# Mamba-2 SSD blocks: decay differences and order mask by TensorE into PSUM, dt on x, eight heads per vector operation

## The chip, the cores and the metric

The program runs on one core of one Trainium2 chip. The metric is the device time of an execution in microseconds. The kernel before took 2283.06 us, the median of three runs (2283.03 to 2285.35).

The core's engines are named as in the profile: PE (TensorE, matrix products; PEld is its loading of weights), DVE (VectorE, element by element), ACT (ScalarE, functions such as exp, and copies), POOL (GpSimd, element by element) and SP (SyncE, which issues the DMAs here). Each works through its own instructions in a fixed order. SBUF is the memory that all of them read; PE writes into PSUM, in banks of 512 fp32 columns.

## What is computed

A backbone of two layers over 512 latent tokens with a prefix of 256 context tokens, `D_MODEL` 1024. The first layer has latent attention and RWKV heads, the second Mamba-2 SSD heads beside windowed attention; each has a ConvFFN after it. The change concerns the SSD scan of the second layer: 16 heads of width 64, in two groups of 8 that share B and C (128 states), both directions in time, chunks of 128 tokens (2 of context, 4 of latents).

```python
a_cum = jnp.cumsum(dtc * a, axis=2)
tri = jnp.tril(jnp.ones((SSD_CHUNK, SSD_CHUNK), bool))
seg = a_cum[:, :, :, None] - a_cum[:, :, None, :]
decay_qk = jnp.exp(jnp.where(tri[:, :, None, None], seg, -jnp.inf))
cb = jnp.einsum('bcqgn,bckgn->bcqkg', cc, bc)
y_diag = jnp.einsum('bcqkgh,bckghp->bcqghp', cb[..., None] * decay_qk * dtc[:, :, None], xc)
decay_end = jnp.exp(a_cum[:, :, -1:] - a_cum)
chunk_states = jnp.einsum('bcqgn,bcqgh,bcqghp->bcghpn', bc, decay_end * dtc, xc)
...
y_off = jnp.einsum('bcqgn,bcghpn,bcqgh->bcqghp', cc, h_in, jnp.exp(a_cum))
y = (y_diag + y_off).reshape(b, l, SSM_HEADS, SSM_P)
```

`y_diag` is the part within a chunk: per head a 128x128 matrix of C·B, times the decay from token k to token q where k is not after q, times `dt` of k. `y_off` is the part from earlier chunks: the state `h_in` at the start of the chunk, read by C and scaled by the decay since then. The direction backwards in time does the same on reversed tokens.

## The kernel before

Activations lie with features on partitions and tokens along the rows. A dense product of the second layer's input projection (`dense`, whose matmuls have line 267, in the helper `mm`) takes a weight tile split into a high and a low part in fp32r (`whi`, `wlo`) and the activations split likewise (`hh`, `hl`), and makes three products per 128 rows of the contraction. The weight tiles are loaded ahead by `load_w` (DMA L322, `whi` on ACT L325, `wlo` on POOL or DVE L326).

PSUM has eight banks in this layer: the pool `acc` with two slots of 1024 columns (two banks each), `sd` with three banks and `b` with one. The dense products of the projections take an `acc` slot; `conv5` (ACT L1225, DVE L1229, SiLU on ACT L1232) drains it, and `token_major` (PE L1238, ACT L1239) transposes the result into `xtm`, x with tokens on partitions.

`decays()` (L1241 to L1279) projects dt for all 32 head-directions onto 48 partitions, makes `ac`, the cumulative decay exponents by two scans (L1257, L1258), and stores them in DRAM as `acd` (L1260). It also makes `dtm` and `acm`, dt and the exponents with tokens on partitions, and `wgt` and `dec` for the states between chunks.

Then, for each group g of 8 heads: four projections of x (`j`); the chain of states over chunks in both directions (`xw` on POOL L1320, a product on PE, `hn` on DVE L1328 and L1330); `cb`, the products of B and C, copied out of PSUM once per direction and multiplied by the mask `le` or `ge` (DVE L1341); and then, for each of the 4 latent chunks c, this (abridged, with the line numbers of the profile):

```
1348  dma(e, acd[c, h0:h0 + 8] broadcast to 128 partitions)
1351  act(gc, e, AF.Exp)
1352  ptt(out=gc, in0=gc, in1=cf[g][:, ls] for 8 heads, op=ALU.mult)
1354  for h in range(8): ts(out=e[:, h], in0=e[:, h], scalar1=acm[...], op0=subtract, op1=min 0)
1356  act(e, e, AF.Exp)
1359  for h in range(8): stt(out=e[:, h], in0=e[:, h], scalar=dtm[...], in1=cb, mult, mult)
```

once for each direction d. A tile of `E` is 128 tokens k by 8 heads by 128 tokens q; a tile of `G` is C with the decay since the chunk's start on it, for 8 heads. Per head, PE then adds four products into one bank of `sd`: for each direction `hn` with `G` (the part from earlier chunks) and `xtm` with `E` (the part within the chunk), each with an output of 64 partitions, the even heads on the lower half and the odd ones on the upper. DVE adds the bank into the output `ym` (L1371). `E` has four buffers, `G` four.

After both groups come the keys, values and queries of the windowed attention (rotary shuffles by DMA, POOL L1383, DVE L1384, L1385, L1390), the gate z (ACT L1548, DVE L1550), and the windowed attention itself.

The order of the instructions on each engine isn't the order of the source. A planner that knows a cost for every instruction sorts them when the program is built: what can start early by its estimate goes early, within the buffers that each tag has. So exponentials of `E` stand on ACT before the projections of x, dense products stand on PE between the SSD products, and the queries' projections and part of the gate's lie among the SSD blocks of group 1. Once built, the order on each engine is fixed; an instruction that isn't ready holds back all that stand behind it.

Of the kernel before, what the change touches and what calls it, by code (L numbers as in the profile page):

```python
# [10 lines left out]
F32 = mybir.dt.float32  # L11
# [6 lines left out]
P = 128  # L18
# [110 lines left out]
def layout(inp):  # L129
# [74 lines left out]
    a["scan2"] = cs["scan2"]  # L204
    a["const1"] = np.concatenate([cs["le"], cs["ge"]], 1)
# [5 lines left out]
def hybrid_kernel(ctx: ExitStack, tc: tile.TileContext, a, out):  # L211
# [1029 lines left out]
    def decays():  # L1241
# [18 lines left out]
        dma(acd.rearrange("c h t -> h c t"), ac[H48].rearrange("p (c t) -> p c t", t=P))  # L1260
        aed = tc.dram_tile([6, 48], F32, name="sp_ae")
# [17 lines left out]
        return acm, wgt, dec, dtm, acd  # L1279

    if DTJ < 0:
        acm, wgt, dec, dtm, acd = decays()
# [20 lines left out]
    seq = ([0, 1, 2, 3, 4, 5], [1, 0, 5, 4, 3, 2])  # L1303
    for g in range(2):
        for j in range(4 * g, 4 * g + 4):
            if j == DTJ:
                acm, wgt, dec, dtm, acd = decays()
# [7 lines left out]
        for d in range(2):  # L1315
            hprev = None
            hs = slice(32 * d + 8 * g, 32 * d + 8 * g + 8)
            for i, c in enumerate(seq[d][:-1]):
                xw = T("sw", [P, 512], "xw", 2)
# [18 lines left out]
        for c in range(2, 6):  # L1338
            for d in range(2):
                cbs[c, d] = T("sw", [P, P], "cb", 8)  # L1340
                tt(out=cbs[c, d], in0=b[:, (c - 2) * P:(c - 1) * P], in1=ge if d else le, op=ALU.mult)  # L1341
        for c in range(2, 6):
            ls = slice((c - 2) * P, (c - 1) * P)
            E, G = [], []
            for d in range(2):
                h0 = 32 * d + 8 * g
                e = T("sw", [P, 8, P], "E", 4)
                dma(e.rearrange("p h t -> p (h t)"),
                    acd[c, h0:h0 + 8].rearrange("h t -> (h t)").unsqueeze(0).partition_broadcast(P))
                gc = T("sw", [P, 8, P], "G", 4)  # L1350
                act(gc, e, AF.Exp)  # L1351
                ptt(out=gc, in0=gc, in1=cf[g][:, ls].unsqueeze(1).to_broadcast([P, 8, P]), op=ALU.mult)
                for h in range(8):
                    ts(out=e[:, h], in0=e[:, h], scalar1=acm[:, c, h0 + h:h0 + h + 1], scalar2=0.0, op0=ALU.subtract,  # L1354
                       op1=ALU.min)
                act(e, e, AF.Exp)
                cb = cbs[c, d]
                for h in range(8):
                    stt(out=e[:, h], in0=e[:, h], scalar=dtm[:, c, h0 + h:h0 + h + 1], in1=cb, op0=ALU.mult,
                        op1=ALU.mult)  # L1360
                E.append(e)
                G.append(gc)
# [263 lines left out]
```

## Time and profile before

| what | value |
|---|---|
| median of three runs | 2283.06 us |
| the profiled execution | 2277.27 us |
| its span, first to last instruction | 2275.6 us |
| mean granted clock of PE | 0.955 |
| PE busy | 2103.0 us |
| DVE busy | 1348.8 us |
| ACT busy | 927.6 us |
| POOL busy | 497.1 us |
| `E` subtractions on DVE (L1354) | 128, 61.1 us |
| `G` products on POOL (L1352) | 16, 39.9 us |
| `E` products on DVE (L1359) | 128, 35.0 us |
| loads of `E` on SP (L1348) | 16 of 512 KB, median 6.6 us to landing |

All times in views of the trace are counted from the start of the span of one profiled execution. A group of instructions is given as line, engine, operation, tiles (written, then read), count, then busy time, the mean of one in ns, and the engine's idle time just before them with what ended it. In a view of stretches each row has a start and an end, its length, the busy time of each engine with the number of instructions, the granted clock of PE (1.00 is full speed) and what the DMA did. An fp32 matmul stands in the trace as two records, an fp32r one as one. In the span the decay blocks of group 0 lie from about 1531 to 1604 us, those of group 1 from about 1643 to 1704 us.

### The profile page before, as it was taken

To read this page: it belongs to the slowest core of one execution; us is meant where nothing else is said; L and a number is where in the kernel's file an instruction comes from. 1 tells how busy PE (TensorE), PEld (TensorE's weight loads), DVE (VectorE), ACT (ScalarE), POOL (GpSimd) and SP (SyncE) were. 2 spreads that over 40 slices of the span, in tenths; PEclk is the share of its full clock that TensorE was granted. 3 is DMA by queue.
4 is the path that set the end of the run, shared out by engine and by line. 5 is a ranking of instruction groups with operands and counts; after the bars stand their busy time and mean duration, and the time that the engine had idled before them with its cause. 6 is when DMAs were issued, how large, how long until landed. Compare 5 with 4: busy or idle time off the path is not lost.

```text
span 2275.6 us, 33862 instructions
## 1 busy us (share of the span) xinstructions
PE 2103.0 (92%) x13558; PEld 1654.7 (73%) x13558; DVE 1348.8 (59%) x2081; ACT 927.6 (41%) x1434; POOL 497.1 (22%) x484
## 2 busy tenths in 40 slices
PE   5988899798899999999999998898888999999997
PEld 3666668686555778888888886786565667888886
DVE  5466865666677556445354454678975556554555
ACT  4345663532245244223132335544344345332434
POOL 0027586621133010000000004342641230000000
PEclk9899899699999999999999999999888999999999
DMA  8477677659861432221211223313426032223231
GB/s 307 110 196 200 176 207 200 208 161 313 256 225 42 148 133 71 61 66 56 74 53 59 75 60 112 97 48 116 132 66 170 31 105 84 93 94 101 84 116 61
DMA packets 181069, 282.58 MB, mean 124 GB/s; under 512 B 63328, under 2 KB 118656, under 8 KB 177840
## 3 DMA queue, kind: packets, MB, share of 16 engines
q1 hardware_dynamic: 180912, 280.42, 40.7%
q8 instruction: 107, 1.75, 0.3%
q14 instruction: 50, 0.41, 0.1%
HBM read 225.43 MB, written 47.33 MB: 120 GB/s over the span
## 4 chain that ended last, share of the span: by engine, by line
PE 64%; DVE 6%; DMA 4%; ACT 4%; issue 2%; SPq 0%; DVEq 0%; POOL 0%; ACTq 0%; POOLq 0%
PE acc L267 49%; PE sd L267 3%; PE wo L267 2%; PE b L267 2%; PE ab L267 2%; PE o L267 2%; DVE E L1354 1%; DMA u<-sp_v 1%; DMA E<-sp_ac 1%; PE ax L267 1%; ACT L416 0%; DMA f<-sp_q 0%; DMA wraw<-w_out 0%; PE mb L267 0%; PE ad L267 0%
## 5 line engine op out<-in xcount | busy, mean ns | idle before, releaser
L267 PE MATMUL acc<-s,whi 128*128 128x512 f32 (+1 forms) x3104 | 762.3, 356 | 2.4 <-ACT s L463 2.4
L267 PEld LDWEIGHTS acc<-s,whi 128*128 128x128 f32 x3104 | 545.1, 188 | 94.3 <-ACT s L463 6.1
L267 PE MATMUL acc<-s,wlo 128*128 128x512 f32 (+1 forms) x1552 | 460.6, 357 | 0.0
L267 PE MATMUL acc<-h,whi 128*128 128x256 f32 (+2 forms) x1248 | 321.6, 371 | 15.4 <-ACT p L635 4.9
L325 ACT CAST whi<-wraw 128x1024 fp32r<-128x1024 f32 (+5 forms) x228 | 210.2, 923 | 284.3 <-PE acc L267 203.9
L267 PEld LDWEIGHTS acc<-s,wlo 128*128 128x128 f32 x1552 | 290.5, 188 | 46.7 <-DVE wlo L326 0.7
L267 PEld LDWEIGHTS acc<-h,whi 128*128 128x128 f32 (+1 forms) x1248 | 223.0, 196 | 67.9 <-issue 15.6
L326 DVE TENSOR_TENSOR wlo<-wraw,whi 128x1024 fp32r<-128x1024 f32 (+5 forms) x205 | 219.2, 1072 | 40.0 <-ACT whi L325 39.4
L381 DVE SCALAR_TENSOR_TENSOR s<-acc,pv,s 128x511 f32<-128x511 f32 (+1 forms) x132 | 87.0, 659 | 245.3 <-ACT s L380 244.4
L380 ACT ACTIVATE s<-acc,pv 128x512 f32<-128x512 f32 (+1 forms) x132 | 93.5, 708 | 231.8 <-PE acc L267 220.5
L484 DVE SCALAR_TENSOR_TENSOR x<-acc,mods,x 128x512 f32<-128x512 f32 (+1 forms) x136 | 79.4, 621 | 176.5 <-PE acc L267 176.4
L267 PE MATMUL acc<-h,wlo 128*128 128x256 f32 (+2 forms) x624 | 179.8, 362 | 0.0
L434 POOL TENSOR_TENSOR f<-f,f 128x768 f32<-128x768 f32 (+1 forms) x24 | 31.3, 1305 | 629.9 <-ACT f L429 622.4
L267 PEld LDWEIGHTS acc<-h,wlo 128*128 128x128 f32 (+1 forms) x624 | 120.3, 196 | 21.7 <-issue 5.2
L383 DVE SCALAR_TENSOR_TENSOR s<-acc,pv,s 128x511 f32<-128x511 f32 (+1 forms) x132 | 87.2, 660 | 4.3
L1173 POOL TENSOR_TENSOR s<-w,s 128x256 f32<-128x256 f32 x6 | 5.0, 857 | 382.4 <-ACT s L416 382.4
L387 ACT CAST s<-s 128x768 fp32r<-128x768 f32 (+1 forms) x44 | 32.0, 727 | 109.4 <-DVE s L1146 109.4
L744 POOL TENSOR_TENSOR w<-I 128x30 f32<-128x30 f32 (+14 forms) x120 | 69.8, 582 | 30.7 <-PE iv L267 12.9
L326 POOL TENSOR_TENSOR wlo<-wraw,whi 128x1024 fp32r<-128x1024 f32 x23 | 62.8, 2734 | 58.5 <-ACT whi L325 55.0
L746 POOL TENSOR_TENSOR I<-I,w 128x30 f32<-128x30 f32 (+14 forms) x120 | 71.9, 599 | 9.1
L1354 DVE TENSOR_SCALAR E<-E,acm 128x128 f32<-128x128 f32 x128 | 61.1, 546 | 16.9 <-ACT G L1351 16.9
L719 DVE TENSOR_TENSOR W<-gk,con 64x512 f32<-64x512 f32 x48 | 32.8, 683 | 55.9 <-ACT PB L718 55.5
(389 smaller groups left out, 3375.0 us busy)
## 6 DMA issues: line engine op xcount, KB each, us to landing
aw<-ada SPq DMA_DIRECT2D x96, 512.0 KB, 6.1
wraw<-up SPq DMA_DIRECT2D x88, 512.0 KB, 3.5
rec<-sp_rec SPq DMA_DIRECT2D x24, 1024.0 KB, 11.4
wraw<-w_in SPq DMA_DIRECT2D x47, 512.0 KB, 3.8
wraw<-down SPq DMA_DIRECT2D x40, 384.0 KB, 3.1
sp_rec<-tg SPq DMA_DIRECT2D x24, 384.0 KB, 3.4
E<-sp_ac SPq DMA_DIRECT2D x16, 512.0 KB, 6.6
x<-xT SPq DMA_DIRECT2D x16, 384.0 KB, 6.0
```

The lines of the kernel that those rows point to most:

```text
L267: ins = nc.tensor.matmul(o, lhsT=lhsT, rhs=rhs, start=start, stop=stop, skip_group_check=shared)
L325: nc.scalar.copy(hi[:, :kt], raw[:, :kt])
L326: (eng or tt)(out=lo[:, :kt], in0=raw[:, :kt], in1=hi[:, :kt].bitcast(F32), op=ALU.subtract)
L380: act(o[rows, t0:t0 + n], ps[rows, po:po + n], AF.Identity, scale=w1, bias=b)
L381: stt(out=o[rows, t0 + 1:t0 + n], in0=ps[rows, po:po + n - 1], scalar=w0, in1=o[rows, t0 + 1:t0 + n], op0=ALU.mult, op1=ALU.add)
L383: stt(out=o[rows, t0:t0 + n - 1], in0=ps[rows, po + 1:po + n], scalar=w2, in1=o[rows, t0:t0 + n - 1], op0=ALU.mult, op1=ALU.add)
L387: nc.scalar.copy(hi, src)
L484: stt(out=x[:, t0:t0 + n], in0=ps[:, po:po + n], scalar=mods[:, c6 * 8 + m, c:c + 1], in1=x[:, t0:t0 + n], op0=ALU.mult, op1=ALU.add)
L719: tt(out=w[hk], in0=b[hk].rearrange("p c (a t) -> p c a t", a=2), in1=mk[hk].rearrange("p (a t) -> p a t", a=2).unsqueeze(1).to_broadcast( ...
L744: eng.tensor_tensor(out=tmp, in0=I[:, m + 1:, m:m + 1].to_broadcast([P, n, m]), in1=I[:, m:m + 1, :m].to_broadcast([P, n, m]), op=ALU.mult)
L746: eng.tensor_tensor(out=I[:, m + 1:, :m], in0=I[:, m + 1:, :m], in1=tmp, op=ALU.add)
L1354: ts(out=e[:, h], in0=e[:, h], scalar1=acm[:, c, h0 + h:h0 + h + 1], scalar2=0.0, op0=ALU.subtract, op1=ALU.min)
```

## The change

- **Decay differences by PE.** `lk[d]` holds 18 rows: the exponents of the 8 heads over the latent tokens, as a high and a low part in fp32r (16 rows, loaded once per group), and two rows of ones. `rq[d]` holds 18 rows by 8 heads by 128 tokens: -1 where a row belongs to the head (a constant, `sel`), and in the last two rows the exponents of the chunk, high and low part, loaded for each chunk and direction. Their product is the difference of the exponents for 8 heads, made in two halves of 512 columns in an `acc` slot.
- **Order mask by PE.** A second product into the same columns, of the identity with `drop[d]`, adds -1e30 where k is after q (before q in the other direction). The exponential is read by ACT straight from PSUM, over 1024 columns. `cb` is copied once per chunk, without a mask.
- **dt on x.** POOL makes `xd`, x times dt, for each chunk and direction; the 8 products by dt on `E` become one of `E` with `cb` over 1024 columns on DVE.
- **Decay of the part from earlier chunks on its products.** `hn` is multiplied with C once for two heads (four products of 128 columns into a bank `z` of `sd`); DVE multiplies the bank by the decays `eg`, which are loaded as a broadcast over 64 partitions for the even and the odd heads and put through an exponential of 512 columns on ACT. The two directions are added on DVE and added into `ym`. `G` is gone.
- **Buffers.** `E` has three, `eg` two, `rq` and `lk` one for each direction, `xw` three, shared by the chain of states and `xd`; `cb` four.
- **In `decays()`** the exponents are split into two fp32r parts and stored in DRAM (`parts`).

```diff
@@ decays() @@
         dma(acd.rearrange("c h t -> h c t"), ac[H48].rearrange("p (c t) -> p c t", t=P))
+        parts = tc.dram_tile([2, 48, NTOK], F32, name="sp_acp")
+        phi, plo = F(F32R), F(F32R)
+        nc.scalar.copy(phi[H48], ac[H48])
+        tt(out=plo[H48], in0=ac[H48], in1=phi[H48].bitcast(F32), op=ALU.subtract)
+        for x, t in enumerate((phi, plo)):
+            dma(parts[x], t[H48].bitcast(F32))
...
@@ before the loop over groups @@
+    idr = T("sw", [P, P], "idr", 1, F32R)
+    nc.scalar.copy(idr, ident)
+    drop = []
+    for d in range(2):
+        m = T("sw", [P, P], f"drop{d}", 1, F32R)
+        ts(out=m, in0=ge if d else le, scalar1=-1.0, scalar2=1e30, op0=ALU.add, op1=ALU.mult)
+        drop.append(m)
+    rq = [T("sw", [18, 8, P], f"rq{d}", 1, F32R) for d in range(2)]
+    lk = [T("sw", [18, NLAT], f"lk{d}", 1, F32R) for d in range(2)]
+    for d in range(2):
+        raw = T("sw", [P, 8, P], "E", 3)
+        dma(raw[0:18].rearrange("p h t -> p (h t)"), a["sel"])
+        nc.scalar.copy(rq[d], raw[0:18])
+        nc.vector.memset(lk[d].bitcast(F32), 1.0)
     for g in range(2):
+        for d in range(2):
+            for x in range(2):
+                dma(lk[d][8 * x:8 * x + 8].bitcast(F32), parts[x, 32 * d + 8 * g:32 * d + 8 * g + 8, L0:L1])
...
-                xw = T("sw", [P, 512], "xw", 2)
+                xw = T("sw", [P, 512], "xw", 3)
...
         for c in range(2, 6):
-            for d in range(2):
-                cbs[c, d] = T("sw", [P, P], "cb", 8)
-                tt(out=cbs[c, d], in0=b[:, (c - 2) * P:(c - 1) * P], in1=ge if d else le, op=ALU.mult)
+            cbs[c] = T("sw", [P, P], "cb", 4)
+            nc.vector.tensor_copy(cbs[c], b[:, (c - 2) * P:(c - 1) * P])
         for c in range(2, 6):
             ls = slice((c - 2) * P, (c - 1) * P)
-            E, G = [], []
+            E, X, Z = [], [], []
             for d in range(2):
                 h0 = 32 * d + 8 * g
-                e = T("sw", [P, 8, P], "E", 4)
-                dma(e.rearrange("p h t -> p (h t)"),
-                    acd[c, h0:h0 + 8].rearrange("h t -> (h t)").unsqueeze(0).partition_broadcast(P))
-                gc = T("sw", [P, 8, P], "G", 4)
-                act(gc, e, AF.Exp)
-                ptt(out=gc, in0=gc, in1=cf[g][:, ls].unsqueeze(1).to_broadcast([P, 8, P]), op=ALU.mult)
-                for h in range(8):
-                    ts(out=e[:, h], in0=e[:, h], scalar1=acm[:, c, h0 + h:h0 + h + 1], scalar2=0.0, op0=ALU.subtract,
-                       op1=ALU.min)
-                act(e, e, AF.Exp)
-                cb = cbs[c, d]
-                for h in range(8):
-                    stt(out=e[:, h], in0=e[:, h], scalar=dtm[:, c, h0 + h:h0 + h + 1], in1=cb, op0=ALU.mult,
-                        op1=ALU.mult)
+                for x in range(2):
+                    dma(rq[d][16 + x:17 + x].bitcast(F32), parts[x, h0:h0 + 8, c * P:(c + 1) * P].unsqueeze(0))
+                eg = T("sw", [P, 4, P], "eg", 2)
+                for par in range(2):
+                    dma(eg[H[par]], acd[c, h0 + par:h0 + 8:2].unsqueeze(0).partition_broadcast(64))
+                act(eg, eg, AF.Exp)
+                ps = acc()
+                for x in range(2):
+                    px = ps[:, x * 512:x * 512 + 512]
+                    mm(px, lhsT=lk[d][:, ls], rhs=rq[d][:, 4 * x:4 * x + 4].rearrange("p h t -> p (h t)"), start=True,
+                       stop=False)
+                    mm(px.rearrange(v4, b=P), lhsT=idr, rhs=drop[d].unsqueeze(1).to_broadcast([P, 4, P]),
+                       start=False, stop=True)
+                e = T("sw", [P, 8, P], "E", 3)
+                act(e.rearrange("p h t -> p (h t)"), ps, AF.Exp)
+                tt(out=e, in0=e, in1=cbs[c].unsqueeze(1).to_broadcast([P, 8, P]), op=ALU.mult)
+                xd = T("sw", [P, 512], "xw", 3)
+                ptt(out=xd.rearrange(h3, x=64), in0=xtm[g][:, c].rearrange(h3, x=64),
+                    in1=dtm[:, c, h0:h0 + 8].unsqueeze(2).to_broadcast([P, 8, 64]), op=ALU.mult)
+                z = sdbank()
+                for j in range(4):
+                    mm(z[:, j * P:(j + 1) * P], lhsT=hin[d, c][:, j * P:(j + 1) * P], rhs=cf[g][:, ls], start=True, stop=True)
+                tt(out=eg, in0=z.rearrange(v4, b=P), in1=eg, op=ALU.mult)
+                Z.append(eg)
+                X.append(xd)
                 E.append(e)
-                G.append(gc)
             b = sdbank()
             for h in range(8):
                 o = b[H[h % 2], (h // 2) * P:(h // 2 + 1) * P]
                 hx = slice(h * 64, h * 64 + 64)
                 for d in range(2):
-                    mm(o, lhsT=hin[d, c][:, hx], rhs=G[d][:, h], start=d == 0, stop=False)
-                    mm(o, lhsT=xtm[g][:, c, hx], rhs=E[d][:, h], start=False, stop=d == 1)
+                    mm(o, lhsT=X[d][:, hx], rhs=E[d][:, h], start=d == 0, stop=d == 1)
             yo = ym[g][:, :, ls]
+            tt(out=Z[0], in0=Z[0], in1=Z[1], op=ALU.add)
+            tt(out=yo, in0=yo, in1=Z[0], op=ALU.add)
             tt(out=yo, in0=b.rearrange(v4, b=P), in1=yo, op=ALU.add)
```

More of the change, by code (lines that the diff above doesn't have):

```diff
@@ L204, in layout @@
     a["scan2"] = cs["scan2"]
+    sel = np.zeros((18, 8, P), np.float32)
+    for h in range(8):
+        sel[h, h], sel[8 + h, h] = -1.0, -1.0
+    a["sel"] = sel.reshape(18, 8 * P)
     a["const1"] = np.concatenate([cs["le"], cs["ge"]], 1)
@@ L1278, in decays @@
         act(dec, dec, AF.Exp)
-        return acm, wgt, dec, dtm, acd
+        return acm, wgt, dec, dtm, acd, parts
     if DTJ < 0:
-        acm, wgt, dec, dtm, acd = decays()
+        acm, wgt, dec, dtm, acd, parts = decays()
     bf, cf, btm = [], [], []
@@ L1303, in hybrid_kernel @@
     seq = ([0, 1, 2, 3, 4, 5], [1, 0, 5, 4, 3, 2])
+    idr = T("sw", [P, P], "idr", 1, F32R)
[12 more added lines that the diff above has]
+        nc.vector.memset(lk[d].bitcast(F32), 1.0)
     for g in range(2):
+        for d in range(2):
+            for x in range(2):
+                dma(lk[d][8 * x:8 * x + 8].bitcast(F32), parts[x, 32 * d + 8 * g:32 * d + 8 * g + 8, L0:L1])
         for j in range(4 * g, 4 * g + 4):
             if j == DTJ:
-                acm, wgt, dec, dtm, acd = decays()
+                acm, wgt, dec, dtm, acd, parts = decays()
             ps = acc()
```

## The prediction

> **What bounds the kernel now.** I read the page first, then the SSD section in stages, then who made TensorE wait there.
>
> ```profile
> span 2275.6 us, 33862 instructions
> PE 2103.0 (92%) x13558; PEld 1654.7 (73%) x13558; DVE 1348.8 (59%) x2081; ACT 927.6 (41%) x1434; POOL 497.1 (22%) x484
> ```
>
> TensorE is busy for 92% of the span, VectorE for 59%. Over the whole kernel a shorter VectorE would buy nothing; the question is whether the edited section is an exception. Busy time by stage (columns: stretch, its length, then busy time of PE, PEld, DVE, ACT, POOL, the granted clock, the DMA share and GB/s):
>
> ```profile
> 1438.00:1448.00 10.00, 1.10 (x6) 0.69 (x6) 4.95 (x23) 5.65 (x6) 0.29 (x1) 0.75 0.82 223
> ...
> 1531.00:1604.00 73.00, 56.31 (x432) 46.39 (x430) 64.36 (x153) 30.07 (x35) 24.20 (x13) 0.90 0.29 92
> ...
> 1643.00:1704.00 61.00, 50.16 (x357) 39.24 (x356) 49.37 (x120) 27.05 (x30) 26.36 (x8) 0.86 0.23 76
> ```
>
> The first row is a hole at the entry, where almost no engine works. The other two are the decay blocks of group 0 and of group 1. In the former DVE is busier than PE, 64.4 of 73 us; in the latter they are level. What TensorE waited for between 1438 and 1704 (us in total, times, longest):
>
> ```profile
> PE sd L267 <- DVE E L1359: 15.1, 4, 8.4
> PE b L1238 <- ACT f L1232: 8.9, 1, 8.9
> PE b L1238 <- ACT f L1239: 6.6, 1, 6.6
> PE sd L267 <- POOL G L1352: 4.1, 1, 4.1
> PE sd L267 <- POOL xw L1320: 3.0, 1, 3.0
> PE b L1238 <- ACT xtm L1239: 1.8, 1, 1.8
> ```
>
> These nine waits carry it. Those on `E` and `G` belong to the decay blocks at once. The 6.6 us put down to a copy on ACT does too:
>
> ```profile
> 1592.63 8.65 DVE L1354 TENSOR_SCALAR E<-E,acm 128x128 f32<-128x128 f32 x8 [1.91 <-ACT G L1351]
> ```
>
> ```profile
> 1601.38 1.06 ACT L1356 ACTIVATE E<-E 128x1024 f32<-128x1024 f32 x1 [6.89 <-DVE E L1354]
> ```
>
> Eight subtractions took 8.65 us on DVE; ACT stood 6.9 us at the exponential behind them, and the copy that TensorE needed was queued on ACT after it. So 15.1 + 6.6 + 4.1 + 1.8 = 27.6 us of TensorE idle time hang on the old decay chain. It costs more than that, since TensorE restarts at half clock (the same columns; the clock is the third last):
>
> ```profile
> 1560.15:1566.00 5.85, 5.85 (x20) 4.84 (x20) 5.85 (x15) 2.73 (x3) 2.52 (x1) 0.51 0.01 3
> 1603.34:1607.00 3.66, 3.66 (x11) 3.04 (x12) 3.56 (x9) 3.35 (x6) 0.00 (x0) 0.52 0.72 206
> 1669.68:1682.00 12.32, 9.86 (x25) 6.36 (x25) 12.32 (x27) 8.22 (x8) 8.88 (x3) 0.50 0.00 0
> 1685.90:1689.00 3.10, 3.10 (x28) 3.10 (x30) 3.10 (x9) 2.40 (x3) 1.25 (x1) 0.53 0.00 0
> ```
>
> PE was busy 5.85 + 3.66 + 9.86 + 3.10 = 22.5 us at about 0.5, so about 11.2 us of that is the slow clock. The decay chain therefore costs 27.6 + 11.2 = 38.8 us of span. That is the most the change can win there.
>
> **VectorE.** Its terms, from the groups of 1531 to 1704 (busy us, mean ns of one, idle before):
>
> ```profile
> L1354 DVE TENSOR_SCALAR E<-E,acm 128x128 f32<-128x128 f32 x96 | 54.3, 635 | 14.8 <-ACT G L1351 14.8
> ...
> L1359 DVE SCALAR_TENSOR_TENSOR E<-E,dtm,cb 128x128 f32<-128x128 f32 x128 | 35.0, 345 | 0.0
> ...
> L1385 DVE TENSOR_TENSOR f<-f,xtm 128x512 f32<-128x512 f32 x5 | 9.6, 1921 | 0.6 <-POOL xtm L1383 0.6
> ...
> L1330 DVE TENSOR_TENSOR hn<-sd,hn 128x512 f32<-128x512 f32 x8 | 5.5, 684 | 0.3
> ...
> L326 DVE TENSOR_TENSOR wlo<-wraw,whi 128x1024 fp32r<-128x1024 f32 x4 | 4.9, 1214 | 1.3 <-ACT whi L325 1.3
> L1550 DVE TENSOR_TENSOR ym<-ym,f 128x512 f32<-128x512 f32 x4 | 4.8, 1220 | 0.0
> ```
>
> The subtractions and the multiplications go: 54.3 + 35.0 = 89.3 us of the 113.7 that DVE worked in the two stages. Added are 16 products of 128x1024 by `cb` (nearest row 1.21 us: 19.4), 16 products of a 512-wide PSUM bank by `eg` (0.68: 10.9), and 16 sums of 128x512 in SBUF (0.68 if alone: 10.9), in all 41.2 us; the copies into `cb` become half as many and lose their mask, which I leave out. The sums read SBUF twice and may be slowed by POOL: L1550 shows 1.22 us, L1385 1.92 us for their size. With sums and products by `cb` stretched by L1550's ratio, 1.22/0.68 = 1.8, the added work is 65.4 us. DVE drops by 24 to 48 us; I take 43, since POOL also loses work. DVE is then no longer the late engine.
>
> **POOL and ACT.** POOL trades the products into `G` for `xd`, which has the shape of L1320; ACT trades an exponential of 1024 per chunk and direction for one of 512:
>
> ```profile
> L1352 POOL TENSOR_TENSOR G<-G,cf 128x1024 f32<-128x1024 f32 x12 | 30.4, 2551 | 63.8 <-ACT G L1351 63.8
> ...
> L1320 POOL TENSOR_TENSOR xw<-xtm,wgt 128x512 f32<-128x512 f32 x10 | 12.5, 1266 | 0.0
> L1351 ACT ACTIVATE G<-E 128x1024 f32<-128x1024 f32 x12 | 12.4, 1051 | 0.0
> ...
> L1551 ACT ACTIVATE f<-ym 128x512 f32<-128x512 f32 x4 | 2.5, 631 | 8.9 <-DVE ym L1550 8.9
> ```
>
> POOL loses 16 x (2.55 - 1.27) = 20.5 us, ACT 16 x (1.05 - 0.63) = 6.7 us. Neither was the path by itself. I cost both at nothing, neither gain nor loss; the cover is TensorE's own work.
>
> **TensorE pays.** Each of the 16 blocks gets four 512-wide fp32r products (two of `lk`, two of the mask) and four 128-wide fp32 products into `z`, and loses eight 64-column products of `hn` with `G`, two records each. Their prices, a stretch of 48 fp32r products, then the four fp32 products of `cb` with the start of what follows them, then a stretch of the 64-column records:
>
> ```profile
> 1426.70:1438.30 11.60, 11.16 (x48) 1.00 0.36 64
> ```
>
> ```profile
> 1529.85 1.05 PE L267 MATMUL sd<-cf,bf 128*128 128x128 f32 x8
> 1530.65 0.47 PE L267 MATMUL acc<-h,wlo 128*128 128x512 f32 x1
> ```
>
> ```profile
> 1651.10:1658.10 7.00, 7.00 (x115) 7.00 (x116) 0.67 (x1) 0.00 (x0) 1.00 0.00 0
> ```
>
> 11.6/48 = 0.24 us each, so 0.97 us for four; 0.80 us for the four of `z`; 7.0/115 = 61 ns a record, so 0.97 us saved for sixteen. Net 0.97 + 0.80 - 0.97 = 0.80 us a block, 12.8 us in all. All of it lies on the path, for TensorE is what the stage is worth once the stalls are gone. `lk` has only 18 rows; an 18-row product could be cheaper than the dense row, at the least free, which bounds the addition at 16 x (0.80 - 0.48) = 5.1 us. I take the dense row, as the columns are the same.
>
> **The new waits.** A block's sums now take one of the two `acc` slots that the dense projections alternate in, from the first `lk` product until ACT has read them: 0.97 + 1.05 us. If the other slot is just being drained, TensorE has the exponential to wait out, 1.05 us by L1351, so up to 16 x 1.05 = 17 us; nothing if `z`, the `E` products or an unfinished dense product fill it. Both must be missing for a wait, and `z` alone is 0.80 us of ready work for 1.05 us: I take a quarter, 4 us. `xd` also takes its buffer from the three of `xw` and holds it until the `E` products are done, so the state chain of the next group can come late at POOL; the old kernel waited 3.0 us for `xw` there, and I leave that wait as it is.
>
> `rq[d]` has one buffer and `eg` two, and each refill is a DMA on SP: two rows and two half broadcasts per block, 64 issues in place of 16, besides `lk`, `sel` and `parts`. SP already waits at such loads (who waited for whom, SP), and the landing times (KB each, median us) are
>
> ```profile
> SPq L1348 <- PE sd L267: 28.0, 6, 12.5
> SPq L1348 <- DVE E L1359: 25.8, 2, 14.5
> ```
>
> ```profile
> xtm<-f SPq DMA_DIRECT2D x20, 64.0 KB, 2.6
> ...
> sp_ae<-ae SPq DMA_DIRECT2D x1, 1.1 KB, 6.9
> ```
>
> The new loads are 4 KB and 128 KB, so they land in 2.6 to 6.9 us; I take 3.5, nearer to the shuffles of `xtm`. An `eg` load for the next chunk waits until `Z[0]` is added into `yo`; behind it on SP stand the other direction's `rq` rows, weight loads and the rotary shuffles. From there to the next such add (start, us for two issues):
>
> ```profile
> 1542.76 0.80 SPq L1348 DMA_DIRECT2D E<-sp_ac  x2
> ```
>
> The ring is 3.5 of landing, 0.97 of sums, 1.05 exponential, 1.21 product by `cb`, 0.68 product by `eg` and 2 x 0.68 adds, with 1.6 us for the four issues at the price of this row, 0.40 us each, 10.4 us a chunk or 42 us a group. The old blocks took 73 and 61 us, so this ring is shorter than what it replaces, and I add nothing for it; if its cover, the dense work beside it, runs out, it shows (a rival below).
>
> **At the entry**, `decays()` gets an ACT copy, a DVE subtraction and two stores ahead of the store of the chunk ends; the first exponentials wait for less data:
>
> ```profile
> 1438.58 1.06 ACT L1351 ACTIVATE G<-E 128x1024 f32<-128x1024 f32 x1 [6.13 <-DMA E<-sp_ac]
> ...
> 1444.43 1.06 ACT L1351 ACTIVATE G<-E 128x1024 f32<-128x1024 f32 x1 [1.67 <-DMA E<-sp_ac]
> ```
>
> Three such landings, of which these are the first and the last, hold ACT up to 1445.5 ahead of the SiLU that TensorE waits 8.9 us for. They follow each other at 5.85/2 = 2.9 us per 0.5 MB, and two buffers of `eg` are 0.5 MB in all, so ACT could be past two such steps, 6 us, earlier; the new steps ahead of it are (0.63 + 0.68) x 768/512 = 2 us. I take 2 us gained, between 6 gained and, if the new steps and one exponential come on top, 3 lost. The one-time loads, copies and mask tiles run beside the dense products of group 0 and cost nothing; without that cover they are two ACT copies of about 1.05 us.
>
> **Sum.** Of the 38.8 us I let 80% go, 31 us, as the order of the instructions is fixed ahead and some waits on `E` will be left. -31 + 12.8 + 4 - 2 = **-16 us**. The profiled execution took 2277.3 us (the span of 2275.6 and 1.7 around it), which becomes 2261; the median of the runs lies 5.8 above that execution, so the forecast is 2283 - 16 = 2267 us.
>
> **A rule against it.** The Trainium skill, page "SBUF — State Buffer", section "Who interferes with whom", says that a VectorE instruction with two SBUF inputs and a GpSimd instruction that reads SBUF contend for one read interface, and that the later one stands still until the earlier one is done. The trace agrees in kind (L1385, 1.92 us where a product out of PSUM of that size takes 0.68), though a mean doesn't tell who held the port. The products by `cb` and the sums are of that kind; where POOL is always first, the time by this rule is that of the contention rival below.
>
> **The rivals.**
> 1. *Slot waits decide (slower).* Place: the `acc` pair. Every block makes TensorE wait out its exponential, 17 us, and the dense products that lose their slot no longer fill the old stalls, of which 60% stay, 15.5 us gained: -15.5 + 12.8 + 17 - 2 = +12, 2295 us. With so much left standing it decides from 5 us of slot waits. For it: two slots, in-order PE. Against: the long dense products are still to be placed around it.
> 2. *The load ring is the stall (no change).* If refills land in 6.9 us, the ring is 13.8 us a chunk, 55 a group, about the old 61: the stalls stay by two thirds, -13 + 12.8 - 2, 2281 us. For it: SP's 25.8 and 28.0 us of waits.
> 3. *Contention keeps DVE late.* All sums and products stretched by L1385's 1.92/0.68 = 2.8: added DVE work (19.4 + 10.9) x 2.8 + 10.9 = 96 us, more than is removed. Half of the stalls stay: -19 + 12.8 + 4 - 2 = -4, 2279 us. Against: POOL loses 20 us.
> 4. *Full recovery.* All 38.8 go, no slot waits, 6 at the entry: -38.8 + 12.8 - 6 = -32, 2251 us.
>
> **How the numbers follow.** Forecast 0.52, rival 1 0.19, rival 2 0.08, rival 3 0.08, rival 4 0.13. About 0.2%, 4.6 us, is what can be told from no change. The forecast is nearly all faster (0.50 of 0.52), as is rival 4; rivals 2 and 3 are mostly within (0.10 of 0.16, 0.04 to faster, 0.02 to slower); so faster 0.67, same 0.12, slower 0.21. The range goes from rival 4 with a little of the cheap `lk` (2247) to just past rival 1 (2296).
>
> **What would show it.** Right: in the stages of the blocks DVE busy falls by some 43 us and waits PE <- DVE E shrink to under 8 us together; PE's records of `ps` and `z` sum to about 28 us at 0.24 and 0.20 each; the clock holds 1.0 there. Wrong: PE waiting on ACT's exponential of `E` over 10 us (rival 1), PE or ACT waiting on loads of `rq` or `eg` (rival 2), products by `cb` over 2 us each (rival 3), or an entry hole longer than 9 us.

## The result, and the profile after

The changed kernel takes 2321.18 us, the median of four runs (2312.36 to 2322.75), beside 2283.05 us (2275.15 to 2285.35) of the kernel before on the same chip: a ratio of 1.0166, 95% interval 1.0138 to 1.0194. It is 38 us slower. The prediction was 2267 us, 16 us faster, with 2296 as the upper end of its range: the sign was wrong, and the range missed too. The profiled execution took 2322.42 us. Of the runs further down, one execution of the last kernel (2806.88 us, at a mean granted clock of 0.67 where its others had 0.95 to 0.96) is left out.

The head of the page (span; busy time of each engine):

```profile
span 2320.6 us, 33672 instructions
PE 2153.8 (93%) x13494; PEld 1678.2 (72%) x13494; DVE 1297.9 (56%) x1870; ACT 925.6 (40%) x1439; POOL 477.0 (21%) x484
```

VectorE fell by 50.9 us and POOL by 20.1, as forecast. Yet the span grew by 45.0 us and TensorE's busy time by 50.8. (Line numbers move: the helper `mm` is L271 now, the exponential of `E` L1390, the product by `cb` L1391, `xd` L1393, the product by `eg` L1398, the adds into `ym` L1409 to L1411, the chain of states L1349 to L1359.)

What TensorE waited for between 1440 and 1720 us, all rows down to 1.1 us (in total, times, longest):

```profile
PE sd L271 <- DVE hn L1359: 11.4, 6, 5.1
PE acc L271 <- DVE f L1233: 6.5, 1, 6.5
PE acc L271 <- ACT E L1390: 5.6, 4, 2.5
PE sd L271 <- POOL xw L1349: 2.3, 7, 0.4
PE b L1242 <- ACT xtm L1243: 1.1, 2, 0.6
```

The waits on `E` of VectorE and on `G` are gone, and the entry hole (second row) is 6.5 us where it was 8.9. The rows sum to 26.9 us; they can't explain 45 us. What is new is the first row: TensorE waits for the chain of states, which had no such row before. Busy time in slices of 10 us around the first of these waits:

```profile
1480.00:1490.00 10.00, 10.00 (x58) 8.28 (x56) 4.92 (x8) 5.17 (x9) 2.40 (x1) 1.00 0.16 52
1490.00:1500.00 10.00, 7.01 (x16) 3.26 (x15) 4.92 (x8) 6.26 (x9) 2.34 (x1) 0.67 0.12 45
1500.00:1510.00 10.00, 9.21 (x17) 4.14 (x17) 0.00 (x0) 4.83 (x6) 2.05 (x3) 0.50 0.03 12
1510.00:1520.00 10.00, 9.14 (x17) 3.29 (x15) 7.80 (x10) 1.17 (x2) 8.73 (x8) 0.81 0.00 0
1520.00:1530.00 10.00, 4.39 (x20) 2.48 (x20) 9.72 (x15) 1.28 (x1) 4.87 (x4) 0.88 0.00 1
1530.00:1540.00 10.00, 9.93 (x64) 7.80 (x64) 6.55 (x9) 3.20 (x4) 3.08 (x2) 0.78 0.18 54
```

The row before 1490 has 58 instructions of TensorE in 10 us; the three behind it have 16 or 17, and the granted clock (the third last column) falls to 0.67 and 0.50. Its busy time hides this: 9.21 of 10 us in the third row. Its own timeline there (start, duration, out<-in, count, idle before and its releaser):

```profile
1488.74 0.60 PE L271 MATMUL acc<-h,whi 128*128 128x256 f32 x2
1489.27 0.49 PE L271 MATMUL acc<-rq,lk 18*128 18x512 f32 x1
...
1493.90 0.79 PE L271 MATMUL acc<-rq,lk 18*128 18x512 f32 x1 [2.52 <-ACT E L1390]
...
1503.76 0.79 PE L271 MATMUL acc<-rq,lk 18*128 18x512 f32 x1
1504.48 0.80 PE L271 MATMUL acc<-drop,idr 128*128 128x512 f32 x1
1505.20 0.79 PE L271 MATMUL acc<-rq,lk 18*128 18x512 f32 x1
...
1509.05 9.05 PE L271 MATMUL sd<-xw,btm 128*128 128x512 f32 x14 [0.22 <-POOL xw L1349]
...
1530.07 2.07 PE L271 MATMUL sd<-cf,hn 128*128 128x128 f32 x8 [5.10 <-DVE hn L1359]
1532.08 3.11 PE L271 MATMUL sd<-E,xw 128*64 128x128 f32 x32
...
1537.46 0.50 PE L271 MATMUL acc<-rq,lk 18*128 18x512 f32 x1
1537.88 0.51 PE L271 MATMUL acc<-drop,idr 128*128 128x512 f32 x1
```

The first row is the last dense product (`acc<-h`) until 1548.5: a stretch of 59 us without one. A second, of 58 us, follows in group 1 (1590.2 to 1647.8). In the kernel before, the longest such stretch among the blocks is 10 us. The sums of two more blocks are written from 1500.86 to 1506.5 and stay in the two `acc` slots until ACT reads them:

```profile
1500.97 1.02 ACT L1390 ACTIVATE E<-acc 128x1024 f32<-128x1024 f32 x1 [2.68 <-PE acc L271]
...
1526.63 1.28 ACT L1390 ACT_TABLE_LOAD   x1 [9.16 <-DVE E L1391]
1535.18 1.94 ACT L1390 ACTIVATE E<-acc 128x1024 f32<-128x1024 f32 x2 [7.27 <-PE sd L271]
```

The third exponential at 1500.97 fills the last of three `E` buffers. The fourth and fifth need a buffer back, so they wait for the first block's `E` products (the releaser is a TensorE product into `sd`, at 1532.08), and these stand behind the chain of states. For 29 us (1506.5 to 1535.18) both slots of `acc` hold finished sums, and every dense product is behind them, in a place where nothing in the view of waits names it.

The whole span, accounted from TensorE's records (busy time while the granted clock stood at a half: 150.7 us before, 215.4 after; half of that is lost):

| TensorE, us | before | after | difference |
|---|---|---|---|
| idle | 172.6 | 166.8 | -5.8 |
| lost to the half clock, up to 1430 us | 53.8 | 65.4 | +11.6 |
| lost to the half clock, behind 1430 us | 21.6 | 42.3 | +20.7 |
| work at full clock | 2027.6 | 2046.1 | +18.5 |
| span | 2275.6 | 2320.6 | +45.0 |

The second row lies ahead of the edited section; over the ten profiles of this case it runs from 53.8 to 76.2, and the 76.2 belongs to the first experiment below, which is faster than the kernel before. By the prediction the other three should have been about -20 (old stalls, slot waits and entry), -9 and +12.8.

Where the 45 us fall can be told too. The last product of the blocks begins at 1700.0 us before and at 1660.5 after: the edited section itself is through 40 us sooner. But it has done less of the dense work on the way. The dense products (those that read `h`) from 1430 us up to that point, before, then after:

```profile
1430.00:1700.00 270.00, 175.34 (x746) 130.69 (x746) 0.00 (x0) 0.00 (x0) 0.00 (x0) 0.91 0.30 94
1430.00:1660.50 230.50, 94.62 (x478) 76.92 (x478) 0.00 (x0) 0.00 (x0) 0.00 (x0) 0.86 0.17 50
```

Of these products 57 are left behind that point before, 347 after. From there to its end the span is 85 us longer: 65 us of work at full clock, 9 of idle time and 10 lost to the half clock. The 290 products that are left over in addition are some 67 us at 0.23 each, about that work. So the loss shows mostly behind the section, as dense work that had lain beside the blocks and now comes later.

### The profile page after: what moved, and what is told of

It reads as the page before. It is cut to its first block, busy times and chain, and to the rows that moved or that the text cites. A ratio compares the mean times of both kernels' runs of the same rounds, so it can differ in the third digit from the quotient of the medians.

```text
span 2320.6 us, 33672 instructions
## 1 busy us (share of the span) xinstructions
PE 2153.8 (93%) x13494; PEld 1678.2 (72%) x13494; DVE 1297.9 (56%) x1870; ACT 925.6 (40%) x1439; POOL 477.0 (21%) x484
## 3 DMA queue, kind: packets, MB, share of 16 engines
q1 hardware_dynamic: 188134, 276.93, 39.5%
## 4 chain that ended last, share of the span: by engine, by line
PE 73%; DMA 7%; DVE 7%; ACT 5%; POOL 4%; issue 3%; SPq 1%; DVEq 0%; ACTq 0%; POOLq 0%
PE acc L271 57%; PE sd L271 3%; PE ab L271 2%; PE wo L271 2%; PE o L271 2%; PE b L271 2%; DMA aw<-ada 2%; DMA u<-sp_v 2%; POOL I L750 1%; POOL w L748 1%; PE gk L271 1%; PE iv L271 1%; PE bkp L271 1%; DMA f<-sp_q 1%; DVE x L466 1%
## 5 line engine op out<-in xcount | busy, mean ns | idle before, releaser
L271 PE MATMUL acc<-s,whi 128*128 128x512 f32 (+1 forms) x3104 | 762.4, 356 | 1.2 <-ACT s L467 1.2
L271 PEld LDWEIGHTS acc<-s,whi 128*128 128x128 f32 x3104 | 544.7, 188 | 92.9 <-ACT s L467 4.2
L271 PE MATMUL acc<-s,wlo 128*128 128x512 f32 (+1 forms) x1552 | 460.8, 357 | 0.0
L271 PE MATMUL acc<-h,whi 128*128 128x256 f32 (+2 forms) x1248 | 310.0, 363 | 19.6 <-DVE f L1233 6.5
L271 PEld LDWEIGHTS acc<-s,wlo 128*128 128x128 f32 x1552 | 290.5, 188 | 47.0 <-DVE wlo L330 0.7
L271 PEld LDWEIGHTS acc<-h,whi 128*128 128x128 f32 (+1 forms) x1248 | 222.2, 196 | 64.5 <-issue 14.6
L271 PE MATMUL acc<-h,wlo 128*128 128x256 f32 (+2 forms) x624 | 175.8, 358 | 0.0
L271 PEld LDWEIGHTS acc<-h,wlo 128*128 128x128 f32 (+1 forms) x624 | 118.7, 194 | 19.3 <-issue 3.0
L330 POOL TENSOR_TENSOR wlo<-wraw,whi 128x1024 fp32r<-128x1024 f32 x23 | 55.5, 2413 | 125.7 <-ACT whi L329 125.4
L1233 DVE SCALAR_TENSOR_TENSOR f<-acc,pv,f 128x254 f32<-128x254 f32 (+3 forms) x80 | 48.5, 614 | 34.9 <-ACT f L1229 33.1
```

The costliest lines, as they stand in the source:

```text
L271: ins = nc.tensor.matmul(o, lhsT=lhsT, rhs=rhs, start=start, stop=stop, skip_group_check=shared)
L330: (eng or tt)(out=lo[:, :kt], in0=raw[:, :kt], in1=hi[:, :kt].bitcast(F32), op=ALU.subtract)
L1233: stt(out=o[:, t0 + lo:t0 + hi], in0=ps[:, po + lo + s:po + hi + s], scalar=col(f"sconv_w{tap}", j), in1=o[:, t0 + lo:t0 + hi], op0=ALU.mu ...
```

## The experiments

Three theories. **A, lock-out**: the sums' slots, held until an `E` buffer is free, shut the dense products out from beside the chain of states. **B, price**: the products of `lk` and of the mask cost TensorE more than the dense product (0.24 us) they were priced by. **C, load ring**: the refills of `rq` and `eg` set the pace. Each ratio is to the kernel before on the same chip, whose median was 2280.90 us beside the first four experiments and 2281.35 beside the last four.

| kernel | median us (runs from, to) | ratio, 95% interval |
|---|---|---|
| changed kernel | 2321.18 (2312.36, 2322.75) | 1.0166, 1.0138 to 1.0194 |
| e1_ps_sd | 2256.68 (2248.32, 2263.14) | 0.9890, 0.9858 to 0.9921 |
| e2_pad | 2309.58 (2302.74, 2310.18) | 1.0115, 1.0088 to 1.0141 |
| e5_oldE | 2266.49 (2262.53, 2269.85) | 0.9934, 0.9914 to 0.9955 |
| e6_sd_pad | 2256.61 (2254.81, 2258.05) | 0.9891, 0.9874 to 0.9909 |
| b1_hold | 2346.62 (2343.85, 2355.12) | 1.0291, 1.0264 to 1.0317 |
| e7_E4 | 2328.25 (2316.18, 2329.08) | 1.0192, 1.0164 to 1.0220 |
| e8_order | 2294.49 (2289.08, 2301.90) | 1.0058, 1.0031 to 1.0085 |
| e9_best | 2261.54 (2254.67, 2266.09) | 0.9911, 0.9888 to 0.9935 |

### The sums out of the `acc` slots (e1_ps_sd)

```diff
-                ps = acc()
+                e = T("sw", [P, 8, P], "E", 3)
                 for x in range(2):
-                    px = ps[:, x * 512:x * 512 + 512]
+                    px = sdbank()
...
-                e = T("sw", [P, 8, P], "E", 3)
-                act(e.rearrange("p h t -> p (h t)"), ps, AF.Exp)
+                    act(e[:, 4 * x:4 * x + 4].rearrange("p h t -> p (h t)"), px, AF.Exp)
```

Each half of the sums goes to one bank of `sd`, with an exponential of its own.

> The sums of the decay exponents go through two one-bank tiles of sd in place of one two-bank acc slot, with an exponential of 512 columns each; nothing else differs from the changed kernel. Theory A (the sums hold both acc slots while they wait for a buffer of E, so the dense products that come after them in the program are locked out for 59 us a group): dense products return between the SSD products, the gap without dense products shrinks from 59 to under 20 us, PE's half-clock stretches around 1495 and 1600 go, and the time falls by 30 to 50 us, to 2270 to 2290. Theory B (TensorE pays more than it was priced at: 0.43 us for each product of the sums where 0.24 was taken, and that is the loss): the time stays within 10 us of 2321. Theory C (the load ring through one rq and two eg buffers is the stall): stays within 10 us of 2321 too, with PE waiting on ACT or DMA in the blocks.

2256.68 us: 64 us below the changed kernel and 24 below the kernel before on its chip (2280.90), with every product and every load of the change still in it. That is 13 us below the range I had given A. The same 59 us of the span:

```profile
1489.00:1548.00 59.00, 58.25 (x316) 45.81 (x317) 40.98 (x64) 29.90 (x45) 24.15 (x17) 1.00 0.14 45
```

TensorE is busy for 58.25 us at full clock with 316 instructions. The changed kernel, over its stretch without dense products:

```profile
1489.30:1548.50 59.20, 48.88 (x188) 27.68 (x187) 35.14 (x46) 20.53 (x27) 24.14 (x18) 0.74 0.09 28
```

And TensorE's timeline in one of the blocks of e1:

```profile
1534.67 0.52 PE L271 MATMUL acc<-h,wlo 128*128 128x256 f32 x2
1535.03 0.28 PE L271 MATMUL acc<-h,whi 128*128 128x256 f32 x1
1535.23 0.49 PE L271 MATMUL sd<-rq,lk 18*128 18x512 f32 x1
1535.65 0.50 PE L271 MATMUL sd<-drop,idr 128*128 128x512 f32 x1
1535.99 0.74 PE L271 MATMUL acc<-h,whi 128*128 128x512 f32 x3
```

Of the dense products from 1430 us on, 16 are left behind the last product of the blocks (at 1695.1 us), where the changed kernel has 347. The sums now stand between dense products, no stretch of over 8 us is without one, and no sum is written before about 1532, when the chain of states is through. The rest of the waits between 1440 and 1700:

```profile
PE acc L271 <- DVE f L1233: 6.2, 1, 6.2
PE sd L271 <- ACT E L1389: 2.1, 2, 1.3
PE sd L271 <- DVE hn L1359: 1.4, 2, 0.8
```

C falls with this: the loads are unchanged and the loss is gone. So does B as the cause of the loss: the price is unchanged too. A is left, but the edit changes the bank, the order and the exponential's width at once; b1 takes the holding by itself and e8 the order. The width has no run of its own.

### The price of the sums (e2_pad, e6_sd_pad)

```diff
-    rq = [T("sw", [18, 8, P], f"rq{d}", 1, F32R) for d in range(2)]
-    lk = [T("sw", [18, NLAT], f"lk{d}", 1, F32R) for d in range(2)]
+    rq = [T("sw", [P, 8, P], f"rq{d}", 1, F32R) for d in range(2)]
+    lk = [T("sw", [P, NLAT], f"lk{d}", 1, F32R) for d in range(2)]
     for d in range(2):
         raw = T("sw", [P, 8, P], "E", 3)
+        nc.vector.memset(raw, 0.0)
...
-        nc.scalar.copy(rq[d], raw[0:18])
+        nc.scalar.copy(rq[d], raw)
```

`lk` and `rq` get 128 rows; those of `rq` behind the 18th are zeros, those of `lk` ones, so the sums are the same. e2_pad is the changed kernel with this, e6_sd_pad is e1 with this.

> lk and rq have 128 rows in place of 18, the added rows of rq being zero; slots as in the changed kernel. This asks why a product of the sums is 0.43 us from the next. If the alternation of 18-row and 128-row weights keeps the weight load (0.19 us) from running under the product before it, the pitch falls to 0.24 us and the time by 64 x 0.19 = 12 us (up to 18 in the half-clock stretches). Theory A: most of that falls in stretches where dense products are locked out and other waits take its place, so 0 to 10 us of gain, 2311 to 2321. Theory B: 12 to 18 us or more, 2303 to 2309. If the pitch stays 0.43 us, the number of rows isn't the reason and the time stays at 2321.

> Both: the sums in sd banks and 128 rows in lk and rq. Theory A with the pitch of 0.24 us: 12 us under the run with the sums in sd alone, about 2262 to 2275, and then faster than the kernel before. Theory B: 12 us under the changed kernel, about 2309. If rows don't set the pitch: as the run with the sums in sd alone.

The records show the price without the waits. In e1 a `lk` product begins 0.42 us (1535.23 to 1535.65) before the mask's, and the dense product follows 0.34 us behind that. In e6:

```profile
1547.40 0.39 PE L271 MATMUL sd<-rq,lk 128*128 128x512 f32 x1
1547.63 0.39 PE L271 MATMUL sd<-drop,idr 128*128 128x512 f32 x1
1547.86 0.40 PE L271 MATMUL sd<-rq,lk 128*128 128x512 f32 x1
```

0.23 us each, the dense row's price. The weight loads show where the time goes. e1, then e6, PEld:

```profile
1546.64 0.19 PEld L271 LDWEIGHTS sd<-drop,idr 128*128 128x128 f32 x1 [0.24 <-issue]
```

```profile
1547.41 0.19 PEld L271 LDWEIGHTS sd<-drop,idr 128*128 128x128 f32 x1
```

Between a weight of 18 rows and one of 128 the load doesn't run under the product ahead of it (0.24 us of idle time, then 0.19 of load); between two of 128 rows it does. The Trainium skill, page "TensorE: Matmul & The Clock Gate", section "LDWEIGHTS (loading the stationary operand)", says that a load's time goes by its columns and not by its rows. The load itself agrees (0.18 us for 18 rows, 0.19 for 128); the spacing of the products doesn't follow from it. Why the load stands still there, no run here tells.

B is thus real: 64 products by at most 0.19 us are up to 12 us, and e2 is 11.6 us faster than the changed kernel. (Its 2309.58 us lies between A's range, from 2311, and B's, up to 2309, and the two intervals, 1.0088 to 1.0141 and 1.0138 to 1.0194, just touch; the spacing of the records is the firmer sign.) But that is under a fifth of the 64 us that e1 gives back, and once the slots are free it isn't worth its own size. Between the end of the entry hole and the first long wait behind the blocks, e1 and e6:

```profile
1453.75:1703.90 250.15, 244.07 (x1345) 186.56 (x1345) 167.66 (x214) 131.74 (x188) 92.88 (x59) 0.99 0.30 95
```

```profile
1446.80:1693.80 247.00, 234.72 (x1345) 187.71 (x1345) 168.96 (x211) 131.43 (x188) 93.51 (x59) 0.99 0.30 96
```

TensorE's busy time falls by 9.4 us and the stretch by 3.2: the rest became idle time in the blocks. The medians are the same (2256.68 and 2256.61), so the 12 us under e1 that I had expected of e6 didn't come. (The profiled execution of e1 is its slowest, 2263.14 us.)

### The old differences, the rest of the change (e5_oldE)

```diff
-                ps = acc()
-                for x in range(2):
...
-                e = T("sw", [P, 8, P], "E", 3)
-                act(e.rearrange("p h t -> p (h t)"), ps, AF.Exp)
+                e = T("sw", [P, 8, P], "E", 4)
+                dma(e.rearrange("p h t -> p (h t)"),
+                    acd[c, h0:h0 + 8].rearrange("h t -> (h t)").unsqueeze(0).partition_broadcast(P))
+                for h in range(8):
+                    ts(out=e[:, h], in0=e[:, h], scalar1=acm[:, c, h0 + h:h0 + h + 1], scalar2=0.0, op0=ALU.subtract,
+                       op1=ALU.min)
+                act(e, e, AF.Exp)
```

The cut is against the changed kernel and abridged. `E` has four buffers and is loaded, subtracted and masked (in `cb`) as before; dt on `xd`, one product by `cb` for eight heads, `z` and `eg` stay.

> Only the decay differences and the mask go back to the old way (broadcast load of E, eight subtractions on DVE, masked cb per direction; no lk, rq, drop, parts); dt on x, the one product by cb per block, z and eg stay. It takes no acc slot in the blocks. Theory A: no lock-out, dense products lie between the blocks as before the change, 2270 to 2290 (DVE loses 35 us of products by dt and gains 19 + 22, so near the time before). Theory C: the eg loads are still there, two buffers, so about 2321 less the 25 us of products of the sums, 2296 to 2310. Theory B: 2321 less the 25 us, 2296.

2266.49 us, 14 below the kernel before and a little below the range I had given A: the part of the change that uses no slot gains by itself. The sums by TensorE, from `sd`, add some 10 us to that (e1; the two intervals just overlap at 0.991 to 0.992); from `acc` they cost 55.

### The slots alone (b1_hold)

```diff
                 gc = T("sw", [P, 8, P], "G", 4)
+                ps = acc()
+                mm(ps[:, :P], lhsT=ident, rhs=cf[g][:, ls], start=True, stop=True)
+                act(gc[:, 0], ps[:, :P], AF.Copy)
                 act(gc, e, AF.Exp)
```

The kernel before, plus one small product per block into an `acc` slot, read out into `G`, where the next instruction overwrites it.

> The kernel before, with no edit of the change in it, but every block of the 16 takes one acc slot, puts one 128-column product of the identity into it and has ACT copy it into G, which the rest of the block overwrites; the slot is thus held until G is free. The added work itself is about 16 x 0.4 us = 6 us of TensorE. Lock-out of the dense products (they stand behind the held slots): TensorE idles and halves its clock beside the blocks, +25 to +45 us, and a stretch of over 30 us without a dense product shows. Price of the sums on TensorE decides: +3 to +8 us, for there are none here. Load ring of rq and eg decides: +3 to +8 us as well.

2346.62 us: 65 us slower than the kernel before, for 16 products of 0.4 us. From 1488.1 to 1548.2 no dense product runs, and again for 60 us in group 1:

```profile
1488.00:1548.00 60.00, 31.37 (x185) 19.22 (x183) 43.59 (x98) 22.70 (x33) 25.71 (x16) 0.74 0.11 35
```

TensorE works 31 of 60 us, at a mean clock of 0.74. The last product that gets a slot there is that of 1509.34, and ACT reads both slots out only when TensorE is through with `G`, 32 us later:

```profile
1541.71 0.54 ACT L1353 ACTIVATE G<-acc 128x128 f32<-128x128 f32 x2 [16.27 <-PE sd L267]
```

This is A without B or C, at more than the 25 to 45 us that I gave it. But there is another cost in it: here TensorE also waits openly for a slot to be drained. ACT's copy and DVE's convolution stand behind exponentials and subtractions of the old decay chain, with no dense product beside them:

```profile
1501.45 0.80 PE L267 MATMUL acc<-cf,con 128*128 128x128 f32 x2 [5.06 <-ACT G L1353]
1509.34 0.80 PE L267 MATMUL acc<-cf,con 128*128 128x128 f32 x2 [7.09 <-DVE f L1229]
```

Waits of this kind sum to 39 us between 1440 and 1740; in the changed kernel those behind the entry are the 5.6 us on `E`. So b1 shows that held slots alone empty the section of dense products, but its 65 us is no measure of what they cost in the changed kernel.

### One more buffer of E (e7_E4)

```diff
-                e = T("sw", [P, 8, P], "E", 3)
+                e = T("sw", [P, 8, P], "E", 4)
```

(also where `sel` is staged.)

> The changed kernel with four buffers of E in place of three. Lock-out: one more block's sums can be read out before the E products of the block three back are done, so a slot is freed one block earlier, yet both slots are still taken by sums ahead of the dense products: 2300 to 2320 us, with a shorter stretch without dense products. If the wait for E is the whole of the lock-out: 2260 to 2280 us. Price of the sums: as the changed kernel, 2319 to 2323 us. Load ring: as the changed kernel.

2328.25 us, no gain, where I had expected 2300 to 2320 and a shorter stretch. So the number of `E` buffers isn't the lever. In the trace four blocks are read out instead of three (the fourth by 1508.4), the next two then take both slots until 1539 to 1541, and the stretches without dense products are 58 and 59 us as before. The sums run ahead as far as the buffers allow, and however far that is, the last two keep the slots until the chain of states and the first block's products are through.

### The order in which the slots are asked for (e8_order)

```diff
+    def xproj(g):
         for j in range(4 * g, 4 * g + 4):
...
+        if g == 0:
+            xproj(0)
         hin = {}
...
+        if g == 0:
+            xproj(1)
         b = sdbank()
         cbs = {}
```

The cut is abridged. Group 1's projections of x stand ahead of group 0's blocks in the program; nothing is added or left out.

> The changed kernel with the x projections of group 1 put ahead of the blocks of group 0 in the program, so that they have the acc slots before the sums ask for them; the number of products and of sums is the same. Lock-out: the order in which the slots are asked for decides, so group 0's state chain gets its dense products back and the hole without them moves to the blocks, which now have none beside them: the time moves by over 10 us in one of the two directions and TensorE's idle time sits in another place. Price of the sums: no change from the changed kernel, within 5 us. Load ring: no change at group 0, within 5 us.

2294.49 us, 27 us below the changed kernel. The dense products are back beside group 0's chain of states (first row). They are now missing in one stretch of 85 us, over the blocks and group 1's chain of states (second row), in place of two stretches of 59 and 58:

```profile
1493.00:1533.00 40.00, 40.00 (x210) 31.45 (x209) 30.27 (x44) 15.58 (x25) 21.73 (x16) 1.00 0.16 53
1533.00:1618.00 85.00, 76.45 (x422) 50.09 (x421) 58.13 (x78) 33.05 (x43) 26.61 (x22) 0.88 0.17 52
```

TensorE loses 8.55 us of the 85 to idle time. The same instructions in another order of asking move the time by 27 us. A expected a move of over 10 us; B and C expected none of over 5, since the sums and the loads are the same.

### All together (e9_best)

e6 with four buffers of `E`.

> The changed kernel with the sums in two one-bank tiles, the rows of lk and rq padded to 128 with zeros, and four buffers of E. No slot of acc is held, so lock-out expects nothing more from the fourth buffer than a microsecond or two: 2252 to 2258 us, as with three. Price of the sums: the same. If E's buffers are what the state chain waits for: 2245 to 2252 us.

2261.54 us, the median of five runs, 3.5 above the range I had given. Its interval contains e6's ratio: a fourth buffer is worth nothing here. The best versions are e1 and e6, 24 us under the kernel before; e1 is the smaller edit.

## Why the prediction was wrong

**The step that failed** is "The new waits". I priced a slot as "the exponential to wait out, 1.05 us", held "from the first `lk` product until ACT has read them: 0.97 + 1.05 us". That assumes ACT can read as soon as the sums are there. ACT needs an `E` buffer to read into, and these come back only when TensorE has used them; the trace shows finished sums in their slots for 29 us. What was then late was not TensorE's next `lk` product but the dense products behind it. I wrote that "the long dense products are still to be placed around it". They were not: the planner let the sums, which are ready early, have both slots first. The term of +4 us became the two stretches of 59 and 58 us, and 347 dense products behind the blocks in place of 57. Moving the sums out of the slots takes 64 us off (e1); holding the slots in the kernel before, with nothing else of the change, adds 65 (b1), 39 of them in open waits.

**Rival 1** had the right place, the `acc` pair, and the right sign. Its price (17 us of exponentials, 60% of the old stalls) was too low by some 26 us, for the same reason. The sign that I named for it, "PE waiting on ACT's exponential of `E` over 10 us", didn't show: 5.6 us. A product that is locked out in the order of the instructions waits without a row of its own; its engine does small things at half clock instead.

**The stalls of the old chain** (38.8 us at most, 31 taken) were there to be won. In e1, where nothing holds the slots, idle time behind 1430 us falls from 67.8 to 39.5 us and the loss to the half clock from 21.6 to 9.0, together 40.9 us. The entry gives 2.7 of that (8.9 to 6.2), so some 38 is left, at the bound of 38.8 rather than at the 31 I took. In the changed kernel the old waits go too, but its own hole takes their place: idle time behind 1430 us falls by 3.2 only, and the half clock costs 20.7 more.

**The price on TensorE** was mis-sized: 0.24 us for each of the four products, measured 0.42 to 0.43 at full clock. With it the step gives 4 x 0.43 + 0.80 - 0.97 = 1.55 us a block, 24.8 in place of 12.8. I took the dense row "as the columns are the same"; I had set a cheaper product as the other bound and none that is dearer. At this price the sum would have been about -4 in place of -16. How much of it reached the span stays open: the account of work shows +18.5 us for the changed kernel but, by the same working, +11.5 for e1, which has the same products.

**What was right.** DVE fell by 50.9 us, forecast 43; the groups between 1440 and 1720 (count, busy us, mean ns):

```profile
L1391 DVE TENSOR_TENSOR E<-E,cb 128x1024 f32<-128x1024 f32 x16 | 22.3, 1430 | 1.1 <-ACT E L1390 1.1
...
L1398 DVE TENSOR_TENSOR eg<-sd,eg 128x512 f32<-128x512 f32 x16 | 10.6, 681 | 5.3 <-PE sd L271 4.3 <-ACT eg L1380 0.9
...
L1409 DVE TENSOR_TENSOR eg<-eg,eg 128x512 f32<-128x512 f32 x8 | 5.5, 692 | 0.3
L1410 DVE TENSOR_TENSOR ym<-ym,eg 128x512 f32<-128x512 f32 x8 | 5.5, 692 | 0.3
```

They sum to 43.9 us; unstretched I had 41.2, and stretched 65.4. The sums took 0.69 us, and rival 3 falls (1.43 us for the products by `cb`, its sign was 2). The slowing by POOL that it rests on is real all the same: of the 16 products by `cb`, the four that began while POOL was in the middle of a product into `xd` took 2.07 us, the others 1.21 to 1.23. In e1 two of the sums began inside an instruction of POOL and took 2.29 and 2.59 us, the others 0.69. The rule of the Trainium skill, page "SBUF — State Buffer", section "Who interferes with whom", gave that rival; these rows agree with it, and the two engines met too seldom for it to decide.

POOL: -20.1, forecast -20.5. ACT: -2.0, forecast -6.7, on no path. The entry: -2.4, forecast -2, by luck: TensorE no longer waits there for ACT behind its exponentials but for DVE, which stood 6.94 us at the load of `dec` (L1286) with the convolution behind it. Rival 2 falls too: no wait of TensorE on a load of `rq` or `eg` stands in the rows above. ACT does wait for loads of `eg`, which I had named as a sign: 14.1 us between 1440 and 1720, but 25.9 in the faster e1.

"The clock holds 1.0 there" came true in e1 (1.00 over the 59 us) and not in the changed kernel.

## What to carry to other kernels

Ask of every buffer that a change shares not how long its work takes but what must happen before it is free again, and follow that to its end: here PSUM slot, `E` buffer, `E` products, chain of states. If ready-early work with a late release shares a pool with the filler that keeps TensorE busy, the filler is locked out and comes later, in time of its own; where the sums are put decides between +38 and -24 us. In the profile, look for the longest stretch without the dense product, for slices with few instructions at a low clock, and count the filler's products beside the section and behind it; the view of waits doesn't name what is not even next in line.

## What was not expected of the hardware

Products of 512 fp32r columns whose weights alternate between 18 and 128 rows follow each other every 0.42 to 0.43 us; with both at 128 rows, every 0.23 (both at full clock). Here zeros for padding are cheaper than fewer rows.

A TensorE that the records show as busy can stay at half clock. The changed kernel, then e2_pad, in the sums ahead of the chain of states:

```profile
1494.00:1507.00 13.00, 12.53 (x22) 5.59 (x22) 3.00 (x4) 6.16 (x8) 0.00 (x0) 0.50 0.12 42
```

```profile
1494.00:1506.00 12.00, 8.27 (x25) 5.72 (x25) 3.00 (x4) 9.49 (x13) 2.29 (x3) 0.72 0.13 46
```

With 18 rows it was busy for 12.53 of 13 us and never left 0.50; the half clock lasted from 1493.4 to 1513.9. With 128 rows it was busy for 69% of the time and came back to full clock within 6.8 us. The Trainium skill, page "TensorE: Matmul & The Clock Gate", section "What's actually happening", lets the clock rise after about 3.4 us of sustained work. The run with 128 rows agrees: TensorE worked without a break from 1498.4 us, and the clock was full at 1501.9, 3.5 us later. The changed kernel doesn't: without a break from 1498.0 to 1507.4, 9.4 us, it stayed at a half. Whether it is the few rows or the weight loads in the open that keep the clock down, no run here tells.
